# Conditioning by halves of the features, and plain float32 products for the small heads of the second block

## The chip, the cores and the metric

The kernel runs on one core of one Trainium2 chip. The metric is the device time of one execution in microseconds (us), as the median of the runs taken. Engines are named as the profile names them: PE is TensorE's matrix products and PEld its loads of the stationary operand, DVE is VectorE, ACT is ScalarE, POOL is GpSimd, SP is SyncE, which issues most transfers. In the profile "L262" is line 262 of the kernel before.

## The reference, cut

Two blocks follow each other on 256 tokens of 1024 features, all in float32, one sequence.

The first block has two hybrid layers. Each takes a conditioning vector (for the tokens and for 256 context tokens) through a 1024 x 3072 product, and gets from it a shift, a scale and a gate for every feature:

```python
shift, scale, gate = jnp.split((sc @ w_ada + b_ada)[:, None, :], 3, axis=-1)
h = rmsnorm(x, norm_w) * (1.0 + scale) + shift
```

`h` then goes through one wide projection into three branches (a gated linear recurrence in four heads, a differential attention in eight heads, a Fourier mixing), which are gated, merged, projected and added to `x` with the gate.

The second block has two layers of mixer, cross attention to 256 memory tokens with four heads of 128, and a gated feed-forward of 2816 features. The mixers differ:

- `mixer_ab` (first layer): two attentions with 8 query heads of 64 on 2 key heads each. The first normalises and rotates its queries and keys; the second only rotates them, has a window of 128 tokens and a sink term in its softmax.
- `mixer_cd` (second layer): an attention of 8 heads of 64 + 32 features whose queries, keys and values come out of low-rank factors, and a neighbourhood attention of 8 heads of 64 with a bias for each relative position.

## The kernel before

**Numbers.** A projection product is made of three products of "reduced" operands (type `F32R`): each operand is split into a high part, its value as that type holds it, and a low part, what is left; `mm3` (lines 259 to 264) multiplies high with high, high with low, low with high, and adds them in PSUM. A weight piece of 128 x 1024 values is read by SP into a ring of three raw buffers (`raw_weights`), its high part is made on ACT (L256) and its low part on DVE or on POOL (L257). The table `POOL` says for each part of the program how many such splits go to POOL: an entry `(n, s)` sends every n-th one there, and n = 0 sends none. `split` (L266 to L274) does the same with activations, always on ACT and DVE. For score products of heads with 64 features, `stack_q` and `stack_k` (L276 to L287) lay the high and the low part of 64 rows over each other in 128 rows, so that two products (`mm_stacked`, L303 and L304) do for three; the low keys stand in tiles whose other half is zero (`make_zeroed`). In the attention of 64 + 32 features and in all value products `mm3` is used.

**Order.** The first block stands in a `tc.block` whose instructions a scheduler orders by a simulated timeline; the second block is issued in the order of the code. Each engine runs its own queue in order. The transfers of weights are all issued by SP in the order of the stream, each as soon as its raw buffer is free.

**Start** (`start`, from L442). SP loads the features of tokens and context (`xT`, 2.1 MB) and 16 pieces of the conditioning weight, 0.5 MB each, in the order of the rows of that weight: two pieces make one row block of 128 input features with all 2048 columns that shift and scale need. They go through four slots in two `big` tiles. For each row block four products of 512 columns (L474), in four column groups of the array, add into one PSUM bank (`pv`), over all eight row blocks. Then the bank is copied, transposed, and the bias is added; then `hybrid_norm` normalises all eight feature blocks, one after the other, splits them, and the first projection can start.

**Conditioning inside the layers.** The gate third of the first layer and all three thirds of the second are made later, in eight places: `ada_product` (from L502) takes a group of 512 columns, reads its four pieces (two row blocks each) through the three raw buffers of the projections, runs two products of 512 columns for each piece (L510), copies the bank to SBUF on ACT, and turns and sums the four column groups by four small products with `sum4`. It is called after heads 1 and 3 of the recurrence branch and after each pair of heads of the attention branch in `hybrid`.

**`mixer_ab`** (from L1366). Token-wise projections give keys and values; keys are normalised (`head_norm`, with the inverse root L335 to L338), rotated (`rope_tok`) and transposed; values are scaled and split into high and low tiles, each head twice side by side. The queries follow, for both attentions. Then, for each of four pairs of heads and both attentions, it computes scores for two blocks of 128 queries, then the softmax and the transposition of the probabilities (`softmax_t`, L1274 to L1307; L1299 scales 256 columns, L1301 transposes), and `pair_values` (from L1312) multiplies by the values and splits the result into the `y` tiles. Between these come the projections of the memory's keys and values (`memory_now`); the output projection ends the mixer.

**`mixer_cd`** (from L1473) makes the low-rank factors first, then, for each of four pairs of heads, both attentions in turn; `near_project` makes the queries and keys of the neighbourhood attention for the next pair.

PSUM has 8 banks of 512 float32 columns for each partition; their names (`mm`, `sc`, `tp`, `pv`) stand as tile names in the profile. Buffer counts of the second block are in `SECOND`.

## Time and profile before

| | |
|---|---|
| median of 3 runs | 2439.83 us (2437.66 to 2440.39) |
| the profiled execution | 2442.6 us, of which its span is 2440.8 |
| PE busy | 2296.8 us, 94% of the span |
| PEld busy | 2066.6 us, 85% |
| DVE busy | 1617.7 us, 66% |
| ACT busy | 1163.4 us, 48% |
| POOL busy | 472.2 us, 19% |
| mean granted clock of PE | 0.977 of full speed |
| DMA | 330.87 MB, 136 GB/s in the mean |

Busy times are sums over the span, so the stages have to be told apart by time. In the trace the start is at 0 to 42 us, the first hybrid layer ends at about 1020, the second at 1661; `mixer_ab` is at 1661 to 1831, its cross attention to 1880, its feed-forward to 2062; `mixer_cd` at 2062 to 2204, its cross attention to 2255, its feed-forward to the end. The granted clock is the share of TensorE's full speed that the throttle allowed; the two levels are 1.2 and 2.4 GHz, so a mean of 0.81 over a stretch says that part of it ran at the lower one. A row of the order in time gives a start, a duration, an engine and a line; "xN" is a burst of N like instructions in one row. In a group by line, what stands behind "|" is the idle time of the engine just ahead of these instructions and what ended most of it.

### The profile page before, as it was taken

How to read it: one execution, taken by the hardware profiler on the slowest of the kernel's cores; microseconds unless marked ns; L12 is line 12 of the kernel's file. 1: busy time of each engine (PE TensorE's matmuls, PEld its weight loads, DVE VectorE, ACT ScalarE, POOL GpSimd, SP SyncE). 2: the span in 40 equal slices, each digit the busy share in tenths (PEclk: the TensorE clock that was granted, in tenths of full speed). 3: DMA queues.
4: the chain of work that ended last, by engine and by line, in shares of the span. 5: the costliest groups of instructions: out<-in, count | busy, mean ns of one | idle time of the engine just before them, and what ended most of it. 6: DMA issues, size and time to landing. Idle time of an engine off the chain costs nothing.

```text
span 2440.8 us, 40377 instructions
## 1 busy us (share of the span) xinstructions
PE 2296.8 (94%) x15566; PEld 2066.6 (85%) x15566; DVE 1617.7 (66%) x3372; ACT 1163.4 (48%) x2172; POOL 472.2 (19%) x354
## 2 busy tenths in 40 slices
PE   6999999999999999989999999898698999888998
PEld 3787878798797887779889999896588999788998
DVE  5745566466575555586557778666987766887765
ACT  3344443444554233335445666444465444665543
POOL 2422220111121102002110000123352211222221
PEclk8999999999999999999999999998899999999999
DMA  6223234323323434443445434554233555433554
GB/s 254 78 92 114 95 109 155 125 88 101 116 93 131 151 103 154 142 130 117 134 147 186 131 113 141 180 166 147 86 102 123 183 183 180 132 109 121 189 183 139
DMA packets 111072, 330.87 MB, mean 136 GB/s; under 512 B 12320, under 2 KB 24352, under 8 KB 110880
## 3 DMA queue, kind: packets, MB, share of 16 engines
q1 hardware_dynamic: 90432, 299.87, 37.5%
q10 hardware_dynamic: 20448, 28.42, 3.4%
q8 instruction: 123, 2.02, 0.4%
...
## 4 chain that ended last, share of the span: by engine, by line
PE 80%; DVE 12%; ACT 3%; DMA 3%; issue 2%; POOL 0%; ACTq 0%; SPq 0%; DVEq 0%; POOLq 0%
PE mm L262 22%; PE mm L263 22%; PE mm L264 22%; PE pv L262 2%; PE pv L263 2%; PE pv L264 2%; DVE w_low L257 1%; DVE h L274 1%; ACT w_high L256 1%; DVE e L1299 1%; DMA w_raw<-wstream 1%; PE mm L510 1%; PE sc L303 1%; DVE mx L1279 1%; PE sc L304 1%
## 5 line engine op out<-in xcount | busy, mean ns | idle before, releaser
L256 ACT CAST w_high<-w_raw 128x1024 fp32r<-128x1024 f32 (+1 forms) x490 | 508.0, 1038 | 583.1 <-PE mm L263 351.8
L257 DVE TENSOR_TENSOR w_low<-w_raw,w_high 128x1024 fp32r<-128x1024 f32 (+1 forms) x395 | 497.3, 1260 | 189.3 <-ACT w_high L256 184.8
L262 PE MATMUL mm<-big,w_high 128*128 128x512 f32 (+1 forms) x1664 | 573.3, 346 | 12.4 <-DVE g L942 5.7
L263 PE MATMUL mm<-big,w_high 128*128 128x512 f32 (+1 forms) x1664 | 571.3, 344 | 0.0
L264 PE MATMUL mm<-big,w_low 128*128 128x512 f32 (+1 forms) x1664 | 570.0, 343 | 0.0
L257 POOL TENSOR_TENSOR w_low<-w_raw,w_high 128x1024 fp32r<-128x1024 f32 x95 | 230.4, 2428 | 739.6 <-ACT w_high L256 600.3
L262 PEld LDWEIGHTS mm<-big,w_high 128*128 128x128 f32 x1664 | 316.1, 190 | 56.6 <-DVE g L942 6.1
L264 PEld LDWEIGHTS mm<-big,w_low 128*128 128x128 f32 x1664 | 316.4, 190 | 37.5 <-DVE w_low L257 0.4
L263 PEld LDWEIGHTS mm<-big,w_high 128*128 128x128 f32 x1664 | 316.6, 190 | 36.5 <-DVE big L271 0.2
L263 PE MATMUL mm<-w_low,big 128*128 128x256 f32 x960 | 269.9, 282 | 4.2 <-POOL w_low L257 2.8
L262 PE MATMUL mm<-w_high,big 128*128 128x256 f32 x960 | 268.0, 282 | 1.6 <-ACT w_high L256 1.6
L264 PE MATMUL mm<-w_high,big 128*128 128x256 f32 x960 | 268.3, 281 | 0.0
L263 PE MATMUL mm<-h,w_high 128*128 128x256 f32 x896 | 255.5, 285 | 4.8 <-DVE h L274 4.1
L262 PE MATMUL mm<-h,w_high 128*128 128x256 f32 x896 | 253.4, 284 | 2.7 <-ACT h L273 1.7
L264 PE MATMUL mm<-h,w_low 128*128 128x256 f32 x896 | 253.6, 283 | 0.0
L263 PEld LDWEIGHTS mm<-w_low,big 128*128 128x128 f32 x960 | 181.1, 189 | 6.2 <-POOL w_low L257 3.7
L262 PEld LDWEIGHTS mm<-w_high,big 128*128 128x128 f32 x960 | 180.6, 189 | 3.5 <-ACT w_high L256 2.8
L264 PEld LDWEIGHTS mm<-w_high,big 128*128 128x128 f32 x960 | 181.0, 189 | 0.4
L263 PEld LDWEIGHTS mm<-h,w_high 128*128 128x128 f32 x896 | 169.7, 189 | 7.6 <-DVE h L274 7.5
L262 PEld LDWEIGHTS mm<-h,w_high 128*128 128x128 f32 x896 | 169.5, 190 | 4.4 <-ACT h L273 2.8
L264 PEld LDWEIGHTS mm<-h,w_low 128*128 128x128 f32 x896 | 169.7, 190 | 0.1
L1649 POOL TENSOR_TENSOR x<-x,r 128x256 f32<-128x256 f32 x44 | 60.2, 1368 | 190.7 <-ACT t L1648 190.7
(475 smaller groups left out, 4388.8 us busy)
## 6 DMA issues: line engine op xcount, KB each, us to landing
...
```

The lines of the kernel that those rows point to most:

```text
L256: nc.scalar.copy(h, raw)
L257: eng.tensor_tensor(lo, raw, h.bitcast(F32), op=ALU.subtract)
L262: nc.tensor.matmul(out, a[0], b[0], start=start, stop=False)
L263: nc.tensor.matmul(out, a[0], b[1], start=False, stop=False)
L264: nc.tensor.matmul(out, a[1], b[0], start=False, stop=stop)
L274: nc.vector.scalar_tensor_tensor(lo, src, scale, h.bitcast(F32), op0=ALU.mult, op1=ALU.subtract)
L303: nc.tensor.matmul(out, q, k[0], start=start, stop=False)
L304: nc.tensor.matmul(out, q, k[1], start=False, stop=stop)
L510: nc.tensor.matmul(ps[j:j + 32], self.sc32[:, 2 * q + k], raw[:, k], start=(q < 2), stop=(q >= 2))
L1279: nc.vector.reduce_max(mx, ps2, axis=AX.X, negate=True)
L1299: nc.vector.tensor_scalar(p[:, u], p[:, u], sm[:, u:u + 1], None, op0=ALU.mult)
L1649: nc.gpsimd.tensor_tensor(g, g, rb, op=ALU.mult)
```

## The change

It has three parts.

1. **Start.** The 16 pieces of the first layer's conditioning come by column groups of 512 instead of by row blocks. A piece now holds two row blocks of one group. The order is shift of the first 512 features, scale of the first 512, shift of the last 512, scale of the last 512, and after each pair `hybrid_norm` is advanced by four feature blocks. Of each seven pieces in turn, four go through slots in one `big` tile, and three through the ring of raw buffers of the projections. The sum over the column groups is made with `sum4`, as in the layers. `hybrid_stats` and the multiplication of the features with their inverse root come after the first group's products.
2. **Conditioning in halves.** `ada_half` takes half of the row blocks of a group: two pieces, four products, each in a column group of its own, put forward by high priority with the other three tied behind the first. The first half's bank is copied to `acc`, and the second half adds it on DVE. There are 16 calls, one after each head, in place of eight.
3. **Second block.** The attentions of both mixers use plain float32 operands instead of split ones: one product for two or three. Queries, keys and values are written by ACT (or by DVE with their scale) without a low part; keys stand in pairs of half-zero tiles, one for each head of a pair; values stand in tiles with columns of zeros between the heads (`between_zeros`), so that both heads of a pair add into the same 256 columns of a bank, and `y` is split once over 128 rows. The projections stay as they are. In both mixers no split of weights goes to POOL any more, and the buffer counts in `SECOND` change.

```diff
-SECOND = dict(load=2, act=16, q=8, p=4, x=4, e=3, s=2, t=3, r=2)
+SECOND = dict(load=2, act=8, vz=4, q=8, p=3, x=4, e=3, s=2, t=3, r=2)
...
 POOL = dict(start=(2, 0), g0=(1, 0), g1=(0, 0), a0=(4, 1), a1=(0, 0), b0=(2, 1), b1=(0, 0), c0=(3, 0), c1=(3, 0),
-            merge0=(0, 0), merge1=(0, 0), t=(4, 2), e=(0, 0), ab=(1, 0), x=(3, 2), cd=(3, 1), f=(0, 0))
+            merge0=(0, 0), merge1=(0, 0), t=(4, 2), e=(0, 0), ab=(0, 0), x=(3, 2), cd=(0, 0), f=(0, 0))
...
+    def make_zeroed_halves(self, n):
+
+        self.zero_tiles, self.n_zero = [], 0
+        for i in range(n):
+            t = [self.pool.tile([P, S], F32, tag=f"kz{i}{u}", name=self.name("kz"), bufs=1) for u in range(2)]
+            for u in range(2):
+                self.nc.gpsimd.memset(t[u][64 * (1 - u):64 * (2 - u)], 0.0)
             self.zero_tiles.append(t)
...
         xc = self.xc = self.big()
-        slots = []
...
+        t = self.big().rearrange("p k c -> p (k c)").rearrange("p (n c) -> p n c", n=4)
+        slots = [t[:, q] for q in range(4)]
...
-        for k in range(KT):
-            nc.vector.tensor_tensor(xc[:, k], xc[:, k], rb, op=ALU.mult)
...
+        norm, n_piece = None, 0
+
+        def piece(g, q):
+            nonlocal n_piece
+            n_piece += 1
+            if n_piece % 7 in (0, 5, 6):
+                return self.raw_weights("w_ada", 0, 2 * q, 2, _cols(512 * g, 512))
+            n = self.stream.add("w_ada", 0, 2 * q, 2, _cols(512 * g, 512))
+            raw = slots[n_piece % 7 - 1]
+            nc.sync.dma_start(raw, self.io["wstream"][n])
+            return raw
+
+        for i in range(2):
+            for g in (i, 2 + i):
+                ps = self.bank("sc")
+                for half in range(2):
+                    raws = [piece(g, 2 * half + q).rearrange("p (k c) -> p k c", k=2) for q in range(2)]
+                    for j in range(4):
+                        nc.tensor.matmul(ps[32 * j:32 * j + 32], self.sc32[:, 4 * half + j], raws[j // 2][:, j % 2], start=(half == 0), stop=(half == 1))
+                if norm is None:
+                    rb = self.hybrid_stats()
+                    for k in range(KT):
+                        nc.vector.tensor_tensor(xc[:, k], xc[:, k], rb, op=ALU.mult)
+                    norm = self.hybrid_norm(0)
+                row = self.u("e")
+                nc.scalar.copy(row, ps)
+                pt = self.bank("tp")[:, :8]
+                for c in range(4):
+                    nc.tensor.matmul(pt[:, 2 * c:2 * c + 2], row[:, c * P:(c + 1) * P], self.sum4, start=True, stop=True)
+                for s in range(2):
+                    o = a[:, 4 * g:4 * g + 4, s]
+                    nc.vector.tensor_tensor(o, pt[:, s:8:2], self.vecs[:, b0 + 4 * g:b0 + 4 * g + 4], op=ALU.add)
+                    if g >= 2:
+                        nc.vector.scalar_tensor_tensor(o, o, 1.0, self.vec("norm_w0")[:, 4 * i:4 * i + 4], op0=ALU.add, op1=ALU.mult)
+            for _ in range(4):
+                next(norm)
+        next(norm, None)
         self.load_consts(CUT_1, self.base, "xres")
...
-    def ada_group(self, l, groups):
-        for g in groups:
-            self.ada_product(l, g)
-
-    def ada_product(self, l, g):
+    def ada_half(self, l, g, half):
 
         nc = self.nc
         ps = self.mm()
-        for q in range(4):
-            raw = self.raw_weights("w_ada", l, 2 * q, 2, _cols(512 * g, 512)).rearrange("p (k c) -> p k c", k=2)
-            for k in range(2):
-                j = 32 * (2 * (q % 2) + k)
-                nc.tensor.matmul(ps[j:j + 32], self.sc32[:, 2 * q + k], raw[:, k], start=(q < 2), stop=(q >= 2))
+        raw = [self.raw_weights("w_ada", l, 4 * half + 2 * q, 2, _cols(512 * g, 512)).rearrange("p (k c) -> p k c", k=2) for q in range(2)]
+
+        def product(j):
+            return nc.tensor.matmul(ps[32 * j:32 * j + 32], self.sc32[:, 4 * half + j], raw[j // 2][:, j % 2], start=True, stop=True)
+
+
+        with self.tc.high_priority():
+            first = product(3)
+            with self.tc.issue_after(first.ins if hasattr(first, "ins") else first):
+                for j in range(3):
+                    product(j)
+        if half == 0:
+            nc.scalar.copy(self.acc, ps)
+            return
         row = self.u("y")
-        nc.scalar.copy(row, ps)
+        nc.vector.tensor_tensor(row, ps, self.acc, op=ALU.add)
...
-            if hd in (1, 3):
-                self.ada_group(l, range(4 + hd // 2, 5 + hd // 2))
+            self.ada_half(l, 4 + hd // 2, hd % 2)
...
                 if last_end:
                     last_end()
+                if l == 0:
+                    self.ada_half(1, pair, u)
                 self.merge_gates(GATES_B)
-            if l == 0:
-                self.ada_group(1, range(pair, pair + 1))
...
-        if whole:
+        if not isinstance(pts, tuple):
+            nc.scalar.copy(pts[:, :, :, sl], pt)
+        elif whole:
             self.split(pts[0][:, :, :, sl], pts[1][:, :, :, sl], pt)
...
-    def pair_values(self, y, k, pts, vs):
-
-        po = self.bank("pv").rearrange("p (u c) -> p u c", u=2)
+    def between_zeros(self, n):
+
+        v = self.u("vz", [P, 64 * (2 * n + 1)])
+        self.nc.gpsimd.memset(v[:, :P * n].rearrange("p (g c) -> p g c", c=P)[:, :, :64], 0.0)
+        self.nc.gpsimd.memset(v[:, P * n:], 0.0)
+        return v, v[:, 64:].rearrange("p (g c) -> p g c", c=P)[:, :, :64]
+
+    def pair_values(self, y, k, pts, v, heads):
+
+        po = self.bank("pv")[:, :S]
         for u in range(2):
-            m = 64 * (u + 1)
+            lo = P * heads[u] + 64 * (1 - u)
             for s in range(2):
-                vh, vl = vs(u, s)
-                self.mm3(po[:m, u], (vh, vl), (pts[0][:, u, s], pts[1][:, u, s]), s == 0, s == 1)
-            rows = slice(64 * u, 64 * u + 64)
-            self.split(y[0][rows, k, :S], y[1][rows, k, :S], po[rows, u])
+                self.nc.tensor.matmul(po, v[s][:, lo:lo + P], pts[:, u, s], start=u == 0 and s == 0, stop=u == 1 and s == 1)
+        self.split(y[0][:, k, :S], y[1][:, k, :S], po)
...
+    def key_tile(self, src):
+
+        k = self.zeroed()
+        for u in range(2):
+            self.nc.scalar.copy(k[u][64 * u:64 * u + 64], src[64 * u:64 * u + 64])
+        return k
...
             nc.scalar.activation(kx, pss[t][:, :256], AF.Copy, scale=r[:, t:t + 1])
-            v = tuple(self.u("act", dt=F32R) for _ in range(2))
...
+            v, at = self.between_zeros(4)
+            nc.scalar.activation(at, pss[t][:, 256:].rearrange("p (g c) -> p g c", c=64), AF.Copy, scale=r[:, t:t + 1])
             vv.append(v)
...
+            kv = kr.rearrange("p (g u c) -> p g u c", u=2, c=64)
+            for i, (kx_, rn) in enumerate(((ka, "r2"), (kb, "r1"))):
+                self.rope_tok([kv[:, 2 * i + g, 0].unsqueeze(1) for g in range(2)], kx_, tab[rn + "_c"][:, t], tab[rn + "_s"][:, t], 2, 32)
+                nc.scalar.copy(kv[:, 2 * i:2 * i + 2, 1], kv[:, 2 * i:2 * i + 2, 0])
...
-        for src in (kt_ps, kt_ps2):
...
+                nc.tensor.transpose((kt_ps, kt_ps2)[g // 2][:, (g % 2) * S + t * P:(g % 2) * S + (t + 1) * P], kr[:, P * g:P * g + P], self.ident)
+
+        kT = [[self.key_tile(src[:, g * S:(g + 1) * S]) for g in range(2)] for src in (kt_ps, kt_ps2)]
...
-                qT[kind].append([self.u("q", dt=F32R) for _ in range(2)])
-                for u in range(2):
-                    self.stack_q(qT[kind][i][u], ptq[i][64 * u:64 * u + 64])
+                qT[kind].append(self.u("q"))
+                nc.scalar.copy(qT[kind][i], ptq[i])
...
-                pts = self.new_pts()
+                pts = self.u("p", [P, 2, 2, S])
...
-                        self.mm_stacked(ps[:, u], qT[kind][pr // 2][u][:, qsl], tuple(x[:, ksl] for x in kT[kind]), kind == 0, kind == 0 or u == 1)
+                        nc.tensor.matmul(ps[:, u], qT[kind][pr // 2][:, qsl], kT[kind][g][u], start=kind == 0, stop=kind == 0 or u == 1)
...
-                self.pair_values(y, 4 * kind + pr, pts, vs)
+                self.pair_values(y, 4 * kind + pr, pts, vv, (2 * kind + g,) * 2)
...
-            t = self.u("x")[:, :S]
-            self.nc.vector.tensor_tensor(t, ps, rb, op=ALU.mult)
...
+            if j == 0:
+                q = self.u("q")[:, :S]
+                self.nc.vector.tensor_tensor(q, ps, rb, op=ALU.mult)
+            else:
+                k = self.zeroed()
+                for u in range(2):
+                    sl = slice(64 * u, 64 * u + 64)
+                    self.nc.vector.tensor_tensor(k[u][sl], ps[sl], rb[sl], op=ALU.mult)
+        return q, k
...
-                v = tuple(self.u("act", dt=F32R) for _ in range(2))
-                self.split(v[0], v[1], pss[t], scale=r[:, t:t + 1])
+                v, at = self.between_zeros(8)
+                nc.scalar.activation(at, pss[t].rearrange("p (g c) -> p g c", c=64), AF.Copy, scale=r[:, t:t + 1])
...
-            c = tuple(self.u("p", [P, 2, S], F32R) for _ in range(2))
+            c = tuple(self.u("q", [P, 2, S], F32R) for _ in range(2))
...
+            v, at = self.between_zeros(8)
+            nc.scalar.copy(at, ps.rearrange("p (g c) -> p g c", c=64))
...
-                a, b = (self.u("q", [P, 2, S], F32R)[:96] for _ in range(2))
-                self.split(a, b, pt)
-                pair.append((a, b))
-            pts = self.new_pts()
+                a = self.u("q", [P, 2, S])[:96]
+                nc.scalar.copy(a, pt)
+                pair.append(a)
...
+            pts = self.u("p", [P, 2, 2, S])
             for qi in range(2):
                 ps = self.bank("sc").rearrange("p (u c) -> p u c", u=2)
                 for u in range(2):
-                    a, b = pair[u]
-                    qsl = slice(qi * P, (qi + 1) * P)
-                    self.mm3(ps[:, u], (a[:, 0, qsl], b[:, 0, qsl]), (a[:, 1], b[:, 1]), True, True)
+                    nc.tensor.matmul(ps[:, u], pair[u][:, 0, qi * P:(qi + 1) * P], pair[u][:, 1], start=True, stop=True)
                 self.softmax_t(ps, pts, qi)
-            self.pair_values(y, pr, pts, lambda u, s, pr=pr: tuple(x[:, P * pr:P * pr + 64 * (u + 1)] for x in vc[s]))
-
-            pts = self.new_pts()
+            self.pair_values(y, pr, pts, vc, (2 * pr, 2 * pr + 1))
...
+            pts = self.u("p", [P, 2, 2, S])
...
-                    self.mm_stacked(ps[:, u * S:(u + 1) * S], qk[u][:, qi * P:(qi + 1) * P], qk[2 + u])
+                    nc.tensor.matmul(ps[:, u * S:(u + 1) * S], qk[0][:, qi * P:(qi + 1) * P], qk[1][u], start=True, stop=True)
...
+            self.pair_values(y, 4 + pr, pts, vd, (2 * pr, 2 * pr + 1))
...
-            a = self.u("act" if f < 16 else "q", [P, 2, S], F32R)
+            if f % 2 == 0 and f < 8:
+                two = self.u("vz", [P, 2, 2, S], F32R)
+            a = two[:, f % 2] if f < 8 else self.u("act" if f < 16 else "q", [P, 2, S], F32R)
```

## Rows read from the trace of the kernel before

**Rows 1.** Page, part 1: busy us (share of the span) xinstructions.

```profile
PE 2296.8 (94%) x15566; PEld 2066.6 (85%) x15566; DVE 1617.7 (66%) x3372; ACT 1163.4 (48%) x2172; POOL 472.2 (19%) x354
```

**Rows 2.** Stretches: busy us by engine, clock, DMA; sums of eight and 26.

```profile
1178.00:1195.00 17.00, 15.44 (x86) 11.60 (x85) 10.55 (x25) 8.68 (x20) 3.49 (x4) 0.81 0.61 202
sum 115.00, PE 96.02 PEld 66.14 DVE 57.68 ACT 61.01 POOL 22.34; mean PE 12.00 PEld 8.27 DVE 7.21 ACT 7.63 POOL 2.79
...
sum 833.00, PE 825.14 PEld 711.88 DVE 490.39 ACT 346.62 POOL 147.29; mean PE 31.74 PEld 27.38 DVE 18.86 ACT 13.33 POOL 5.66
```

**Rows 3.** Stretches of the two mixers, columns as before.

```profile
1679.00:1738.00 59.00, 40.45 (x169) 31.82 (x167) 49.15 (x101) 23.39 (x40) 24.19 (x10) 0.83 0.33 107
1738.00:1797.00 59.00, 46.18 (x297) 39.86 (x297) 55.11 (x131) 38.75 (x116) 16.75 (x8) 0.94 0.17 54
...
2100.00:2180.00 80.00, 67.63 (x476) 60.33 (x475) 65.66 (x127) 59.70 (x156) 18.04 (x14) 0.94 0.35 113
```

**Rows 4.** Groups by line, 1660 to 1830 us: busy us, mean ns | idle before.

```profile
L1299 DVE TENSOR_SCALAR e<-e,sm 128x256 f32<-128x256 f32 x32 | 20.1, 663 | 0.2
L274 DVE SCALAR_TENSOR_TENSOR h<-xres,vecs,h 128x256 fp32r<-128x256 f32 x15 | 17.9, 1225 | 3.9 <-ACT h L273 3.9
L271 DVE TENSOR_TENSOR p<-tp,p 128x512 fp32r<-128x512 f32 x16 | 10.7, 682 | 1.4 <-ACT p L270 1.3
L338 DVE TENSOR_TENSOR hn_r_t<-hn_r_t,hn_r_v 128x2 f32<-128x2 f32 x6 | 7.4, 1236 | 0.2
...
L257 POOL TENSOR_TENSOR w_low<-w_raw,w_high 128x1024 fp32r<-128x1024 f32 x26 | 62.4, 2403 | 98.6 <-ACT w_high L256 89.3 <-DMA load<-rpb 5.6 <-PE pv L264 3.8
```

**Rows 5.** Chain of waits, 1738 to 1840 us: start us, us, what.

```profile
1774.82 0.22 PE tp L1301 x2
1784.54 0.52 DVE e L1299 x2
```

**Rows 6.** Order in time, 1680 to 1700 us: start us, us, engine, line.

```profile
1681.95 2.37 POOL L257 TENSOR_TENSOR w_low<-w_raw,w_high 128x1024 fp32r<-128x1024 f32 x1 [0.43 <-ACT w_high L256]
1681.97 2.36 DVE L338 TENSOR_TENSOR hn_r_t<-hn_r_t,hn_r_v 128x2 f32<-128x2 f32 x1
1684.76 0.16 DVE L338 TENSOR_TENSOR hn_r_t<-hn_r_t,hn_r_v 128x2 f32<-128x2 f32 x1
1685.03 0.48 DVE L274 SCALAR_TENSOR_TENSOR act<-mm,rstd,act 128x256 fp32r<-128x256 f32 x1
```

**Rows 7.** Stretch from 4 to 40 us, columns as in rows 2.

```profile
4.00:40.00 36.00, 21.09 (x84) 6.65 (x84) 21.45 (x56) 9.65 (x15) 7.86 (x3) 0.91 1.03 400
```

**Rows 8.** Order in time, 37 to 43 us.

```profile
37.81 1.05 PE L474 MATMUL pv<-big,sc 128*32 128x512 f32 x4 [0.23 <-DMA big<-wstream]
42.15 0.79 PE L262 MATMUL pv<-big,w_high 128*128 128x512 f32 x1 [1.89 <-ACT big L270]
```

**Rows 9.** Order in time, TensorE, 216 to 226 us.

```profile
216.49 1.91 PE L510 MATMUL mm<-w_raw,sc 128*32 128x512 f32 x12
221.72 1.05 PE L510 MATMUL mm<-w_raw,sc 128*32 128x512 f32 x4 [1.02 <-DMA w_raw<-wstream]
```

**Rows 10.** Chain of waits, 216 to 226 us.

```profile
216.56 1.02 PE mm L510 x8
217.59 4.09 DMA w_raw<-wstream
```

**Rows 11.** Order in time, TensorE, 2300 to 2303 us.

```profile
2300.40 0.28 PE L262 MATMUL mm<-h,w_high 128*128 128x256 f32 x1
2300.51 0.28 PE L263 MATMUL mm<-h,w_high 128*128 128x256 f32 x1
```

**Rows 12.** Order in time, TensorE, 803 to 806 us.

```profile
803.31 1.05 PE L357 MATMUL tp<-ident,b_rs 128*128 128x128 f32 x8
804.12 0.48 PE L264 MATMUL mm<-big,w_low 128*128 128x512 f32 x1
```

**Rows 13.** Order in time, TensorE, 1140 to 1180 us.

```profile
1144.74 0.69 PE L872 MATMUL sc<-negm,ident 4*128 4x256 f32 x2
```

58 lines of the change are left out of this document (3 added, 55 removed).

## The prediction

> **What bounds the kernel now.** I read the engine totals and slices first: TensorE is busy 94% of the span, so only a stretch in which it stands still or runs slowly can give time back [rows 1]. The table by stretch says where these are. Most of the first block is not among them: in 26 stretches of it, 833 us, TensorE is busy for 825 [rows 2]. What is left is the start (no projection product until 42 us), the eight places where a conditioning product of 512 columns runs (TensorE busy 96.0 us of 115) [rows 2], and the mixers of the second block: `mixer_ab` from 1679 us on, where VectorE is busy 49 of 59 us and then 55 of 59, and the attention part of `mixer_cd`, where it is busy 66 of 80 [rows 3]. Then I grouped what VectorE does there. Its scaling of 256 columns (L1299) takes 663 ns in the mean, the 2-column step L338 of the inverse root 1236 ns (a second row, of 8 columns, has six more of 1252) [rows 4], while undisturbed ones take 0.26 us (two in 0.52 in the chain [rows 5]) and 0.16. The order in time shows why: GpSimd starts a split of 2.37 us at 1681.95, VectorE starts a 2-column step at 1681.97, and both end together; the next step of that form takes 0.16 us [rows 6]. So a GpSimd split holds a VectorE step that comes behind it for the split's whole length. The profiled run took 2442.6 us (span 2440.8); the median of the runs is 2439.8, 2.8 less. The sum is made against 2442.6.
>
> **Start.** The transfers run at 400 GB/s from 4 to 40 us without a gap [rows 7], so bytes set this part. The last of 16 conditioning pieces is used at 37.81, and the first product with a projection weight starts at 42.15 [rows 8]. Now every piece has to be there before the first feature is normalised. After: features (2.1 MB), vectors (0.35) and 16 pieces (8.4) are 10.9 MB; with 0.5 MB moved by 4 us they are there at 4 + 10.4/0.40 = 30 us. The first half is there at 4 + 6.1/0.40 = 19 us, and its four features are multiplied and split (about 1.5 us each on VectorE) while the second half arrives. The first weight follows at 31, its cast takes 1 us, so products start at about 33, with 4 features times 3 products in up to 4 banks to do (48 products, 11 us) while the other features come, at 33 to 38. That is 9 us earlier. Bounds: 3 us if the constants, memory and three weights stand in front as they do now (then only the normalisation is hidden), 14 if weights come between the halves. The 64 records of this conditioning on TensorE stay and lie under the transfers.
>
> **Conditioning in halves.** A product now takes a burst of 12 records (1.91 us) and a burst of 4 (1.05) for the fourth piece, which needs the buffer of the first [rows 9]: the chain shows 4.09 us for that transfer at 217.59 [rows 10]. Afterwards a half has two pieces for which three buffers are there, and its four products, in four column groups, make one burst of 8 records, which takes 1.02 us now [rows 10]. TensorE: from 8 x 2.96 = 23.7 to 16 x 1.05 = 16.8 us, 6.9 less. Idle: 19.0 us now [rows 2]. But the half's first product, put forward by high priority, stands at the head of TensorE's queue, and all projection products behind it, and the casts and evictions that wait for them, are late if the second piece is. The waits of that kind seen are 0 to 1.65 us; I take 0.8 for each of 16, 13 us, so 6 less. A granted clock below 1 at three of the eight, as at 1178 (0.81) [rows 2], gives about 1 more. Sum 14 less; bounds 24 less (idle 4, clock full) and 4 more (16 waits of 1.8 and no clock regained). The eight additions of 512 columns that VectorE gets for ACT copies (6 us) have cover in the first block, where it is busy some 60%; without cover they cost 6.
>
> **The plain float32 products.** Today three (or two, stacked) reduced products of 256 columns start every 0.117 us [rows 11]; 512 columns take twice that. A plain product shows as two records: eight records of 128 columns (four products) take 1.05 us, and the next product starts 0.81 us after the first of them [rows 12]; doubled to 256 columns that is 0.41 to 0.52 us each, while the two records L872 of 256 columns and 4 rows take 0.69 [rows 13]. I take 0.44, near the first since its operands are of full height, and keep 0.41 and 0.69. Counts are from the loops. `mixer_ab`: 64 score products become 32 (7.5 to 14.1 us), 96 value products become 32 (11.2 to 14.1): 9.5 more. `mixer_cd`: 48 become 16, 32 become 16, 96 become 32: 20.6 to 28.2, 7.6 more. TensorE pays 17 us; at 0.69 it is 49.
>
> **What `mixer_ab` gets for it.** VectorE loses 16 subtractions L271 of 512 columns (10.7 us [rows 4]), and by the durations of such sizes 12 us more on `y`, `q`, `kz` and the values: 23. GpSimd's 26 splits of 2.40 us move to it at about 1.27, 33 us. The stalls go: L1299 20.1 against 32 x 0.26, L274 on `xres` 17.9 against 15 x 0.48 [rows 6], both rows of L338 14.9 against 12 x 0.17, about 35 us, and 42 with smaller ones [rows 4]. So VectorE is relieved by 23 + 42 - 33 = 32 us, but TensorE then sets the stage. From 1679 to 1738 VectorE's chain rules: 49.2 less 18.6 of those stalls, less 6.1 removed, plus 10 splits (12.3) is 37, with 8 of gaps 45: 14 less than 59. From then TensorE has scores 14.1, masks 1.8, transposes 7 (two in 0.22 [rows 5]), values 14.1, memory products 22.5 and the output projection 22.5: 82 us, and 6 for the first and last links make 88, against 93 now. Together 20 less (bounds 8, with the chain giving 8 and the dearest product eating the rest, and 30). New ACT copies (keys in halves, doubled `kr`) equal those removed. The memsets of value tiles have no row; they are few, on a GpSimd that is freed of 62 us: nothing, and at most 2 us per mixer if each stalls VectorE once as long as its own split would.
>
> **`mixer_cd`.** In its attention stretch VectorE drops 20 us of subtractions of the same forms, some 4 in the near projections and 5.6 of stalls, and takes about 4 splits (5): 66 to some 41. TensorE has about 61 us of work there by the same rates; with gaps the stretch takes 68 instead of 80. A microsecond more comes from splits in the first part that stall small steps. 13 less, bounds 4 (product at 0.69) and 20.
>
> **Sum.** 9 + 14 + 20 + 13 = 56: 2442.6 - 56 = 2387 against the profiled run, 2384 against the median. `act` with 8 tiles and `vz` with 4 hold the arrays that 16 held. One `p` tile fewer touches `cross` alone, where a late low part would wait for one value product, under 1 us. I count both at nothing.
>
> **A rule against it.** The page Perfetto Trace Analysis of the Trainium skill (Optimizing Scalar/DVE Operations) says that a saturated DVE may gain by offloading work to GpSimd, though it warns of a port that both share. By its first half, taking 36 splits back onto a VectorE that is 93% busy loses time; the trace so far bears out the warning, with 42 us of stalls [rows 4, 6], and cannot show the other side.
>
> **Rivals.** (1) VectorE becomes the bound: 36 splits at 1.27 us, 45 us, land in front of the chains' small steps, and both mixers stay as long as now. Then 23 us are gained: 2417. For it: 55 of 59 us [rows 3]. Against it: the pair at 1681.95 [rows 6]. (2) The start and the halves do nothing, since as many bytes stand in front of the last feature and each half waits for its piece: 33 us gained, 2407. For it: the full transfers [rows 7]. (3) Slower: the half's first product, at the head of TensorE's queue, waits for a whole transfer. At the 4.09 us of 217.59, 16 halves lose 66 us, and a clock that drops after each, at 1.5 us, 24 more; less the 26 of today's conditioning and 42 from elsewhere that is 2462. It decides from 2.8 us per half with that clock, 4.3 without. Against it: three raw buffers for two pieces. (4) The plain products cost 0.69 each: 32 us more, 2416.
>
> **How the numbers follow.** Forecast 2384, chance 0.66 (2360 to 2402); the second rival 0.14; the first and fourth together 0.14; slower 0.04; no change 0.02. The range leaves out slower and no change and thin tails on both sides: 2356 to 2419. Faster by over 0.2% (5 us, about what a measurement of this kernel can tell) 0.94, within 0.02, slower 0.04.
>
> **What would show it.** First projection product near 33 us; L510's successor in 16 bursts of about 1.05 us, with under 1 us of idle in front; L338 and L1299 in `mixer_ab` at 0.17 and 0.26 us; no GpSimd splits there; score products of about 0.44 us; TensorE above 95% from the first scores to the end of the output projection. Wrong would be: VectorE over 90% busy in `mixer_ab`, conditioning products waiting 2 us or more for a transfer, plain products above 0.6 us.

## The result and the profile after

The changed kernel takes 2377.26 us in the median of 4 runs (2375.91 to 2379.83); the kernel before took 2439.7 beside it. The ratio is 0.9747, with a 95% interval of 0.973 to 0.9764. The forecast was 2384, with 2356 to 2419 as its range. The profiled execution took 2378.5 us (span 2376.7), 64.1 less than the one of before, for a sum of 56.

The totals of the page of the changed kernel answer to [rows 1]: TensorE is busy for 9 us less in a span 64 us shorter, GpSimd for 71 us less.

```profile
PE 2287.5 (96%) x15514; PEld 2064.3 (87%) x15514; DVE 1562.9 (66%) x3340; ACT 1146.0 (48%) x2137; POOL 401.4 (17%) x336
```

To see where 64 us went I cut both traces at the end of the last residual addition of each stage on VectorE (L1262 before, L1288 after; for the first block the last L1006 or its successor). In the trace of the changed kernel the last addition of the first mixer is this one; it ends at 1780.0.

```profile
1779.58 0.42 DVE L1288 TENSOR_TENSOR xres<-mm,xres 128x256 f32<-128x256 f32 x1
```

Lengths of the stages in us, worked out in this way for every profiled execution that the text needs (names of the experiments as below):

| kernel | first block | `mixer_ab` | cross | feed-forward | `mixer_cd` | cross | feed-forward |
|---|---|---|---|---|---|---|---|
| before | 1661.2 | 167.9 | 43.4 | 188.0 | 138.2 | 44.2 | 188.1 |
| after | 1633.5 | 146.5 | 43.8 | 187.6 | 123.6 | 43.8 | 187.6 |
| halves_only | 1631.8 | 164.6 | 43.4 | 189.2 | 137.7 | 44.3 | 188.0 |
| second_only | 1660.3 | 147.0 | 43.4 | 187.7 | 123.9 | 43.5 | 187.6 |
| pool_only | 1657.2 | 144.0 | 42.3 | 188.0 | 132.8 | 43.5 | 188.0 |
| plain_pool_back | 1630.6 | 166.0 | 43.5 | 187.7 | 127.1 | 43.6 | 187.7 |
| ab_split | 1631.0 | 144.2 | 42.5 | 187.6 | 123.5 | 43.7 | 187.7 |
| pool_none | 1627.0 | 147.1 | 40.8 | 187.7 | 123.4 | 40.8 | 187.7 |
| both | 1627.2 | 144.1 | 40.8 | 187.7 | 123.5 | 40.8 | 187.7 |

So 27.7 us came in the first block (start and halves), 21.4 in `mixer_ab`, 14.6 in `mixer_cd`. One pair of traces leaves some 3 us open in `mixer_ab`: with the second block of before it took 167.9 us in the trace of before, but 164.6 in that of halves_only and 164.3 in that of start_only. Against these two the gain in `mixer_ab` is 18 us. The row of halves_only for this stage (from, to, us, then busy us of PE, PEld, DVE, ACT, POOL, clock, DMA):

```profile
1631.80:1796.40 164.60, 131.09 (x765) 112.39 (x765) 132.67 (x280) 89.33 (x199) 70.32 (x34) 0.91 0.32 108
```

**The start.** Order in time, changed kernel; it answers to [rows 8]:

```profile
27.09 0.33 SPq L563 DMA_DIRECT2D load<-memT  x1
34.65 1.82 PE L493 MATMUL sc<-big,sc 128*32 128x512 f32 x4 [0.67 <-DMA big<-wstream]
38.23 4.70 POOL L257 TENSOR_TENSOR w_low<-w_raw,w_high 128x1024 fp32r<-128x1024 f32 x2 [35.59 <-ACT w_high L256]
38.92 0.77 PE L262 MATMUL pv<-big,w_high 128*128 128x512 f32 x1
40.65 3.72 DVE L674 TENSOR_SCALAR s<-big,ada 128x256 f32<-128x256 f32 x5
```

The first projection product (L262) comes at 38.92 for 42.15. The last conditioning piece is used at 34.65, not at 30: SP put the constants (at 10.15) and memory transfers (the second at 27.09) between the pieces. Two GpSimd splits then run for 4.70 us from 38.23, and VectorE's normalisation of the second half of the features (L674) stretches beside them.

**The halves and the plain products.** Order in time of the changed kernel: a burst of a conditioning half, which answers to [rows 9], and a burst of eight records (four value products) in plain float32. The row after it is from the chain of waits, which follows the same burst without the pipeline's overlap at its end.

```profile
212.19 1.06 PE L527 MATMUL mm<-w_raw,sc 128*32 128x512 f32 x8
1704.49 1.89 PE L1353 MATMUL pv<-p,vz 128*128 128x256 f32 x8
```

```profile
1704.65 1.73 PE pv L1353 x8
```

All 16 halves are bursts of 1.06 to 1.07 us, and no conditioning product waits for a transfer: the view of line 527 has 3.9 us of idle time in front of them in all, 3.3 of it without a releaser. A plain product of 256 columns takes 1.73 / 4 = 0.43 us.

**VectorE in `mixer_ab`.** Groups by line, 1633 to 1783 us (busy us, mean ns), which answer to [rows 4]:

```profile
L274 DVE SCALAR_TENSOR_TENSOR h<-xres,vecs,h 128x256 fp32r<-128x256 f32 x16 | 11.4, 745 | 0.8 <-ACT h L273 0.8
L1325 DVE TENSOR_SCALAR e<-e,sm 128x256 f32<-128x256 f32 x32 | 10.0, 349 | 0.4
L347 DVE TENSOR_TENSOR hn_r_t<-hn_r_t,hn_r_v 128x2 f32<-128x2 f32 x6 | 1.0, 159 | 0.2
```

The 2-column step fell from 1236 to 159 ns, the scaling of 256 columns from 663 to 349, the undisturbed step in this count; the 0.26 us of [rows 5] leave out the part in which two in a row overlap. Most of the stalls are gone, as forecast. The scaling of the residual fell from 1225 only to 745, where 0.48 us was forecast. The order in time shows it stretched beside another GpSimd instruction that stayed, the addition of 256 columns L388:

```profile
1761.27 0.48 DVE L274 SCALAR_TENSOR_TENSOR h<-xres,vecs,h 128x256 fp32r<-128x256 f32 x1
1763.77 1.07 POOL L388 TENSOR_TENSOR acc<-acc,t 128x256 f32<-128x256 f32 x1 [71.79 <-ACT t L387]
1764.16 0.96 DVE L274 SCALAR_TENSOR_TENSOR h<-xres,vecs,h 128x256 fp32r<-128x256 f32 x1
```

Whether the plain products had a part in the gain, this trace can't say, since both edits came together.

### The profile page after: what moved, and what is told of

It reads as the page before. It is cut to its first block, busy times and chain, and to the rows that moved or that the text cites. A ratio compares the mean times of both kernels' runs of the same rounds, so it can differ in the third digit from the quotient of the medians.

```text
span 2376.7 us, 40209 instructions
## 1 busy us (share of the span) xinstructions
PE 2287.5 (96%) x15514; PEld 2064.3 (87%) x15514; DVE 1562.9 (66%) x3340; ACT 1146.0 (48%) x2137; POOL 401.4 (17%) x336
## 4 chain that ended last, share of the span: by engine, by line
PE 85%; DVE 6%; ACT 3%; DMA 3%; issue 1%; POOL 0%; ACTq 0%; SPq 0%; DVEq 0%; POOLq 0%
PE mm L262 24%; PE mm L263 24%; PE mm L264 24%; PE pv L263 1%; PE pv L262 1%; PE pv L264 1%; DVE w_low L257 1%; ACT w_high L256 1%; PE pv L1353 1%; PE sc L312 1%; PE tp L366 1%; PE sc L313 1%; PE tp L1182 1%; PE tp L1327 1%; PE mm L527 1%
## 5 line engine op out<-in xcount | busy, mean ns | idle before, releaser
L257 DVE TENSOR_TENSOR w_low<-w_raw,w_high 128x1024 fp32r<-128x1024 f32 (+1 forms) x429 | 533.7, 1245 | 221.6 <-ACT w_high L256 218.0
L262 PE MATMUL mm<-big,w_high 128*128 128x512 f32 (+1 forms) x1664 | 573.8, 346 | 14.9 <-ACT y L978 4.7
L262 PEld LDWEIGHTS mm<-big,w_high 128*128 128x128 f32 x1664 | 315.9, 190 | 60.4 <-ACT s L1212 5.6
L262 PE MATMUL mm<-w_high,big 128*128 128x256 f32 x960 | 267.9, 281 | 0.0
L262 PE MATMUL mm<-h,w_high 128*128 128x256 f32 x896 | 253.5, 284 | 4.6 <-ACT h L273 2.0
L257 POOL TENSOR_TENSOR w_low<-w_raw,w_high 128x1024 fp32r<-128x1024 f32 x61 | 148.4, 2434 | 542.5 <-ACT w_high L256 466.7
L262 PEld LDWEIGHTS mm<-w_high,big 128*128 128x128 f32 x960 | 179.7, 188 | 1.2
L262 PEld LDWEIGHTS mm<-h,w_high 128*128 128x128 f32 x896 | 168.4, 188 | 6.2 <-ACT h L273 2.9
L918 POOL TENSOR_TENSOR e<-e,s 128x256 f32<-128x256 f32 (+3 forms) x68 | 65.1, 969 | 178.8 <-ACT e L917 178.7
```

The lines of the kernel that those rows point to most:

```text
L257: eng.tensor_tensor(lo, raw, h.bitcast(F32), op=ALU.subtract)
L262: nc.tensor.matmul(out, a[0], b[0], start=start, stop=False)
L918: nc.gpsimd.tensor_tensor(e, e, place(sc, s, lo, hi), op=ALU.mult)
```

## The experiments

Each kernel was timed in five rounds beside the kernel before on the same chip; ratios are to that kernel, with a 95% interval. A difference of two runs is made from their ratios, times 2439 us.

### The parts alone

**start_only** is the kernel before with `start` of the changed one.

```diff
-                n = self.stream.add("w_ada", 0, k, 1, _cols(CW * i, CW))
...
-        for _ in self.hybrid_norm(0):
-            pass
...
+            n = self.stream.add("w_ada", 0, 2 * q, 2, _cols(512 * g, 512))
...
+        for i in range(2):
+            for g in (i, 2 + i):
...
+            for _ in range(4):
+                next(norm)
```

> The kernel before with the new start alone (pieces by columns, first half of the features first). Theory A, from aligning the two traces by the number of projection products done: the first product starts 3.2 us earlier, but by 140 us both traces have done the same work within 1 us, because TensorE then waits for the gate chain of the first recurrence and runs at the lower clock behind it. It gives 0 to 3 us: 2437 to 2440. Theory B: the start moves all later transfers forward, so part of the gain seen at the conditioning products comes from here: 8 us or more, 2431 or less.

Measured: 2443.3 us, ratio 1.002 (1.0007 to 1.0034). It is not faster; if anything 2 to 8 us slower, which neither theory had. Counting the projection products done by a given time, its trace is between 2 and 3 us ahead at 60 us, about 1 at 120, level with the one of before at 1520, and 2.4 behind at the end of the first block (1663.6 for 1661.2). The loss comes between 1526 and 1590 us, far from the start; what makes it is open.

**halves_only** is the kernel before with the 16 calls.

```diff
-            if hd in (1, 3):
-                self.ada_group(l, range(4 + hd // 2, 5 + hd // 2))
+            self.ada_half(l, 4 + hd // 2, hd % 2)
...
+                if l == 0:
+                    self.ada_half(1, pair, u)
                 self.merge_gates(GATES_B)
-            if l == 0:
-                self.ada_group(1, range(pair, pair + 1))
```

> The kernel before with the conditioning in halves alone (16 calls of two pieces in place of 8 of four). Theory A: the wait for the fourth piece goes with the burst of 12 records and the second of 4, TensorE loses 6.9 us of records and 15 us or more of idle time, and the clock that fell behind these waits stays up: 24 to 29 us, 2411 to 2416. Theory B: the new start had moved the transfers forward, and the halves alone wait as I forecast, 0.8 us each: 14 us, 2426.

Measured: 2409.62 us, ratio 0.9885 (0.9868 to 0.9903), 28 us. Theory A: the halves alone give all that the first block gained. What TensorE did from 130 us to the end of the first block stands in the sums of the stretches (length, then busy us by engine), of the kernel before:

```profile
sum 1531.00, PE 1484.05 PEld 1321.86 DVE 972.36 ACT 712.49 POOL 226.76; mean PE 371.01 PEld 330.46 DVE 243.09 ACT 178.12 POOL 56.69
```

and of halves_only:

```profile
sum 1502.00, PE 1471.48 PEld 1317.77 DVE 969.12 ACT 712.01 POOL 232.20; mean PE 367.87 PEld 329.44 DVE 242.28 ACT 178.00 POOL 58.05
```

29 us shorter: TensorE is busy for 12.6 us less and idle for 16.4 less (47.0 to 30.5).

**second_only** has the second block of the changed kernel behind the first block of before.

```diff
-SECOND = dict(load=2, act=16, q=8, p=4, x=4, e=3, s=2, t=3, r=2)
+SECOND = dict(load=2, act=8, vz=4, q=8, p=3, x=4, e=3, s=2, t=3, r=2)
...
-            merge0=(0, 0), merge1=(0, 0), t=(4, 2), e=(0, 0), ab=(1, 0), x=(3, 2), cd=(3, 1), f=(0, 0))
+            merge0=(0, 0), merge1=(0, 0), t=(4, 2), e=(0, 0), ab=(0, 0), x=(3, 2), cd=(0, 0), f=(0, 0))
...
-                self.make_zeroed(4)
+                self.make_zeroed_halves(4)
...
-    def pair_values(self, y, k, pts, vs):
+    def pair_values(self, y, k, pts, v, heads):
```

> The kernel before with the changes of the second block alone (plain float32 products, no weight splits on GpSimd in the two mixers). Theory A: the second block stands alone behind the first, so its gain is the 21 us of the first mixer and the 15 us of the second that the traces show: 36 us, 2404. Theory B: a part of it depends on what is loaded ahead at the end of the first block, and alone it gives under 30 us, 2410 or more.

Measured: 2404.99 us, ratio 0.9867 (0.9849 to 0.9884), 32 us; by stages 20.9 and 14.3 against the trace of before. That lies between the theories: the interval, 28 to 37 us, holds A's 36 and the upper end of B. With start_only and halves_only the three parts alone make 5 - 28 - 32 = -55 of the -62 measured together; the rest lies inside the intervals.

### What a conditioning piece holds up

**halves_together** calls both halves of a group one behind the other at the eight old places.

```diff
-            self.ada_half(l, 4 + hd // 2, hd % 2)
+            if hd in (1, 3):
+                for u in range(2):
+                    self.ada_half(l, 4 + hd // 2, u)
...
-                if l == 0:
-                    self.ada_half(1, pair, u)
                 self.merge_gates(GATES_B)
+            if l == 0:
+                for u in range(2):
+                    self.ada_half(1, pair, u)
```

> The changed kernel with both halves of a group called one behind the other at the eight old places. Four pieces are wanted within one call again, with three buffers. Theory A: the wait for a transfer in front of the second half comes back at most of the eight places, 1 to 2.5 us each with the lower clock behind it: 8 to 20 us slower than the changed kernel, 2385 to 2397. Theory B: the bursts of 8 records and the priority did it, and the distance between halves is nothing: 2375 to 2380.

**no_priority** leaves the order of a half's four products to the scheduler.

```diff
-        with self.tc.high_priority():
-            first = product(3)
-            with self.tc.issue_after(first.ins if hasattr(first, "ins") else first):
-                for j in range(3):
-                    product(j)
+        for j in range(4):
+            product(j)
```

> The changed kernel, the four products of a conditioning half issued in their plain order, without the high priority and without being tied behind the last of them. Theory A: what counts is that a half needs two pieces while three buffers are there; the scheduler finds a place of the products in any case, but bursts may break in two: 0 to 6 us slower, 2377 to 2383. Theory B: the priority is what keeps TensorE from waiting, and without it half of the gain of the halves goes: 12 us or more, 2389 or more.

Measured: halves_together 2393.16 us, ratio 0.9815 (0.9795 to 0.9836), 17 us slower than the changed kernel: the size of theory A. But not in its place: the conditioning products of that trace wait for a transfer for 0.5 us in all. no_priority 2382.62 us, ratio 0.9778 (0.9754 to 0.9801), 8 us slower, between the theories, with an interval that just overlaps that of the changed kernel. In its profiled execution only 2.3 us of this show in the first block (1635.8 us for 1633.5).

A likely place is SP's queue. These rows are from the waits of the queue of weight transfers (L242) from 130 to 1300 us, for raw buffers that conditioning products still hold: us in total, times, longest. The kernel before, halves_together, no_priority, the changed kernel, and halves_only:

```profile
SPq L242 <- PE mm L510: 139.1, 22, 19.6
```

```profile
SPq L242 <- PE mm L527: 130.5, 15, 17.7
```

```profile
SPq L242 <- PE mm L527: 53.6, 19, 7.0
```

```profile
SPq L242 <- PE mm L527: 27.5, 11, 4.7
```

```profile
SPq L242 <- PE mm L505: 27.0, 10, 5.0
```

A piece of conditioning lies in one of the three raw buffers until its products have had their turn on TensorE. When that buffer's turn comes, SP, which issues in order, can't send for the next weights, up to 19.6 us at a stretch before. The two kernels with the short first block have 27 us of this wait, the two with the long one over 130, no_priority lies between. But the sum is not the time lost: SP waits for raw buffers most of the time in every one of these kernels, and all its L242 rows together make 1027 us (before), 1021, 1026, 1009 and 1010 of the 1170 us. What sets the slow two apart is who holds the buffer and how long at a stretch: 19.6 and 17.7 us, where no single wait of the other three is over 14.2. So this queue as the cause fits the runs and is not shown; a kernel with a fourth raw buffer, which would test it, was not run. What TensorE then waits for is named otherwise at each place: a cast of a late weight, a softmax that had no projection to hide it. In the sum of the stretches halves_together (130 us to the end of the first block) is idle for 39.8 us of 1517, 9 more than halves_only, and busy for 6 more.

```profile
sum 1517.00, PE 1477.19 PEld 1322.85 DVE 979.81 ACT 713.57 POOL 223.97; mean PE 369.30 PEld 330.71 DVE 244.95 ACT 178.39 POOL 55.99
```

So it is the distance between two halves that counts: without it 17 of the 28 us are lost. For the priority the two intervals leave anything from about nothing to some 15 us.

### The mixers: who made the gain

**pool_only** changes two entries of the table and nothing else.

```diff
-            merge0=(0, 0), merge1=(0, 0), t=(4, 2), e=(0, 0), ab=(1, 0), x=(3, 2), cd=(3, 1), f=(0, 0))
+            merge0=(0, 0), merge1=(0, 0), t=(4, 2), e=(0, 0), ab=(0, 0), x=(3, 2), cd=(0, 0), f=(0, 0))
```

> The kernel before with one table entry changed in each mixer of the second block: no split of weights on GpSimd there, all on VectorE; products and values as before. Theory A: the stalls behind GpSimd's splits (some 42 us of VectorE in the first mixer and 19 in the second) cost more than the 33 and 12 us of splits that VectorE takes over, and VectorE's chain sets both stages: 6 to 16 us faster, 2424 to 2434. Theory B: the splits on VectorE land in front of the small steps of the chain and eat it all, or more: no change or slower, 2438 to 2455; then the plain products are what made room.

**plain_pool_back** is the changed kernel with these entries as before.

```diff
-            merge0=(0, 0), merge1=(0, 0), t=(4, 2), e=(0, 0), ab=(0, 0), x=(3, 2), cd=(0, 0), f=(0, 0))
+            merge0=(0, 0), merge1=(0, 0), t=(4, 2), e=(0, 0), ab=(1, 0), x=(3, 2), cd=(3, 1), f=(0, 0))
```

> The changed kernel with weight splits of both mixers of the second block back on GpSimd as before (all of the first mixer's, every third of the second's). Theory A: the stalls of VectorE's small steps come back, but VectorE has fewer subtractions to do and TensorE more products, so it costs less than the stalls' sum: 5 to 20 us slower than the changed kernel, 2382 to 2397. Theory B: the plain products made the room and the place of the splits no longer matters: 2375 to 2380.

**ab_split** is the changed kernel with the split operands of before in `mixer_ab`, four `p` tiles, and the splits on VectorE.

```diff
-SECOND = dict(load=2, act=8, vz=4, q=8, p=3, x=4, e=3, s=2, t=3, r=2)
+SECOND = dict(load=2, act=8, vz=4, q=8, p=4, x=4, e=3, s=2, t=3, r=2)
...
+            vt = self.u("vz", [P, 2, 512], F32R)
+            v = vt[:, 0], vt[:, 1]
...
+        kh, kl = (self.u("vz", [P, 2, 512], F32R) for _ in range(2))
...
-                        nc.tensor.matmul(ps[:, u], qT[kind][pr // 2][:, qsl], kT[kind][g][u], start=kind == 0, stop=kind == 0 or u == 1)
+                        self.mm_stacked(ps[:, u], qT[kind][pr // 2][u][:, qsl], kT[kind][g], kind == 0, kind == 0 or u == 1)
...
-                self.pair_values(y, 4 * kind + pr, pts, vv, (2 * kind + g,) * 2)
+                self.pair_values_split(y, 4 * kind + pr, pts, vs)
```

> The changed kernel with the split (three and two product) operands of the kernel before in the first mixer of the second block; weight splits on VectorE there, the second mixer plain as changed. Theory A, from the stage lengths of the runs so far (144.0 us with the table entry alone, 146.5 with the plain products too): once the splits are off GpSimd, TensorE sets this mixer, and the plain products cost it 9.5 us of which 2 to 8 show: 2369 to 2375. Theory B: VectorE sets it still, and the 23 us of subtractions that come back make it 5 us slower or more: 2382 to 2395.

Measured: pool_only 2410.53 us, ratio 0.9894 (0.9877 to 0.9912), 26 us faster than before and more than theory A had. plain_pool_back 2399.06 us, ratio 0.9839 (0.9819 to 0.986), 22 us slower than the changed kernel, just past theory A's end. ab_split 2373.4 us, ratio 0.9742 (0.9728 to 0.9755): 1 us faster than the changed kernel by the ratios, which is no difference by itself, but `mixer_ab` in its trace is 2.3 us shorter, the same 144 us as in pool_only.

The whole of `mixer_ab`, as one stretch (us, then busy us of PE, PEld, DVE, ACT, POOL, clock, DMA). The kernel before:

```profile
1661.00:1829.00 168.00, 133.28 (x764) 113.93 (x765) 134.31 (x279) 89.27 (x199) 70.12 (x34) 0.89 0.32 105
```

pool_only, the table alone:

```profile
1657.00:1801.00 144.00, 125.94 (x754) 107.97 (x755) 124.83 (x304) 88.51 (x199) 11.05 (x9) 0.91 0.37 122
```

plain_pool_back, the plain products without the table:

```profile
1630.60:1796.60 166.00, 140.68 (x733) 117.18 (x733) 113.01 (x246) 84.48 (x193) 71.33 (x37) 0.90 0.32 106
```

the changed kernel, with both:

```profile
1633.50:1780.00 146.50, 131.03 (x722) 110.81 (x723) 108.30 (x269) 84.32 (x193) 12.54 (x11) 0.93 0.37 120
```

Here is the case in four lines. From the first to the second VectorE takes over 25 splits (it makes 27 now, 33.6 us by its group below, where it made two in 2.7 us), and is busy for 9.5 us less; 24 us are gained, or 20 against the two other traces with the second block of before. From the first to the third VectorE is relieved of 21 us by the plain products, and the stage is 2 us shorter, or 1 to 2 longer than in those two: nothing that can be told from none. From the second to the fourth it is relieved of 16.5 us again, TensorE has 5.1 more, and the stage is 2.5 us longer. That is little, but it repeats: of the traces without GpSimd splits in this stage, the three with split operands (pool_only, ab_split, both) take 144.0 to 144.3 us in it, the seven with plain ones 146.5 to 148.8.

A split on GpSimd takes twice as long as on VectorE, so the gain could also come from low parts that TensorE gets sooner. The chain of waits speaks against it. In the kernel before it has no GpSimd split in this stage, and no wait of TensorE there was ended by one; VectorE has 102 of its 167 us, the stalled steps in front. In pool_only VectorE has 32 of 144. The beginnings of its sums by line, the kernel before and then pool_only:

```profile
by line: DVE e L1299 9.8%; DVE h L274 9.6%; DVE hn_r_t L338 8.6%; PE mm L264 7.6%; PE mm L262 7.2%; PE mm L263 6.8%; DVE mx L1279 4.9%; issue 4.4%; DVE p L271 3.0%; DVE q L280 2.5%; DVE t L1330 2.4%; ACT h L273 2.3%; DVE x L1337 1.9%; DVE t
```

```profile
by line: PE mm L263 12.1%; PE mm L262 11.9%; PE mm L264 11.7%; DVE w_low L257 6.5%; ACT w_high L256 5.5%; issue 5.3%; ACT e L1286 3.8%; PE tp L1301 3.8%; DMA w_raw<-wstream 3.7%; DMA load<-memT 3.2%; DVE h L274 2.9%; PE sc L303 2.1%; PE pv 
```

Once the stalls are gone, VectorE's own work hardly sets this stage any more, and taking it away buys nothing here.

The groups of pool_only, 1657 to 1801 us, show the same step lengths as the changed kernel, without a plain product:

```profile
L257 DVE TENSOR_TENSOR w_low<-w_raw,w_high 128x1024 fp32r<-128x1024 f32 x27 | 33.6, 1244 | 9.0 <-ACT w_high L256 8.8
L271 DVE TENSOR_TENSOR p<-tp,p 128x512 fp32r<-128x512 f32 x16 | 10.8, 687 | 0.7 <-ACT p L270 0.2
L1299 DVE TENSOR_SCALAR e<-e,sm 128x256 f32<-128x256 f32 x32 | 10.0, 347 | 0.1
L338 DVE TENSOR_TENSOR hn_r_t<-hn_r_t,hn_r_v 128x2 f32<-128x2 f32 x6 | 0.9, 158 | 0.1
```

In `mixer_cd` it is otherwise: by the table of stages the entry alone gives 5.4 us, the plain products alone 10.6 (halves_only to plain_pool_back), both 14.6. That fits a stage in which VectorE's own subtractions, and not stalls, were the larger part of its chain, since only every third split was on GpSimd; this I read from the counts and did not test further.

### The start, and the splits elsewhere

**no_start** is the changed kernel with the start of before.

```diff
-            n = self.stream.add("w_ada", 0, 2 * q, 2, _cols(512 * g, 512))
...
-            for _ in range(4):
-                next(norm)
...
+                n = self.stream.add("w_ada", 0, k, 1, _cols(CW * i, CW))
...
+        for _ in self.hybrid_norm(0):
+            pass
```

> The changed kernel with the start of the kernel before (pieces by rows, all features normalised at its end); the rest as changed. Theory A, from the run with the new start alone (no faster than before): the earlier first product is lost again by 140 us, so the start is worth nothing: 2373 to 2379. Theory B: beside the halves the new start is worth its 3 us, and the kernel is 2 to 5 us slower: 2379 to 2382.

Measured: 2374.75 us, ratio 0.9753 (0.9736 to 0.9771), against 0.9747: no difference. The first block ends at 1633.0 us, against 1633.5. The new start is worth nothing that shows here.

**late_consts** makes SP issue the constants and two memory transfers behind the last piece that goes through a slot.

```diff
+            self.last_piece = d.ins if hasattr(d, "ins") else d
...
-        self.load_consts(CUT_1, self.base, "xres")
+        with self.tc.issue_after(self.last_piece):
+            self.load_consts(CUT_1, self.base, "xres")
...
+                with self.tc.issue_after(self.last_piece):
                     self.b_setup()
...
+                with self.tc.issue_after(self.last_piece):
                     self.memory_stats()
```

> The changed kernel, SP issuing the constants, the lambda vectors and the first memory transfers (1.28 MB until 28 us) behind the last of the conditioning pieces that go through the slots. Theory A: bytes set the start, at 0.40 MB per us, so the last piece lands 3 us earlier (31.5 us for 34.6) and the first projection product starts at some 36 us; at the end of the kernel 0 to 3 us are left of it: 2374 to 2378. Theory B: constants that come late hold up the gate chain of the first recurrence, and the kernel is 1 to 6 us slower: 2378 to 2383.

Measured: 2377.78 us, ratio 0.9753 (0.9732 to 0.9773): no difference. The order in time has the last conditioning products in a burst that ends at 32.86, 3.6 us before that of the changed kernel (34.65 + 1.82):

```profile
30.27 2.59 PE L494 MATMUL sc<-big,sc 128*32 128x512 f32 x8
```

so bytes do set the arrival. But the chain of waits goes elsewhere:

```profile
23.63 10.10 DMA consts<-consts
33.76 0.23 DVE rope_c L1074
```

VectorE's queue is in order, and the products for the rotation tables (L1074) stand in front of the second half of the features: they wait for the constants until 33.73. The first projection product starts at 37.04, for 38.92: about half of what the pieces gained, the constants take.

**pool_none** takes the last 62 splits off GpSimd.

```diff
-POOL = dict(start=(2, 0), g0=(1, 0), g1=(0, 0), a0=(4, 1), a1=(0, 0), b0=(2, 1), b1=(0, 0), c0=(3, 0), c1=(3, 0),
+POOL = dict(start=(0, 0), g0=(0, 0), g1=(0, 0), a0=(0, 0), a1=(0, 0), b0=(0, 0), b1=(0, 0), c0=(0, 0), c1=(0, 0),
...
-            merge0=(0, 0), merge1=(0, 0), t=(4, 2), e=(0, 0), ab=(0, 0), x=(3, 2), cd=(0, 0), f=(0, 0))
+            merge0=(0, 0), merge1=(0, 0), t=(0, 0), e=(0, 0), ab=(0, 0), x=(0, 0), cd=(0, 0), f=(0, 0))
```

> The changed kernel with no split of weights on GpSimd anywhere: the 55 of the first block and the seven of the cross attentions and others go to VectorE too. Theory A, that a GpSimd split holds VectorE's small steps wherever they meet: but TensorE is busy 1585 of the 1633 us before the first mixer, so only part of the 48 us of idle time and of the clock behind it can come back: 2 to 12 us faster, 2365 to 2375. Theory B: VectorE has cover in the first block, and 55 splits of 1.25 us on it come in front of the low parts that TensorE waits for: 0 to 15 us slower, 2377 to 2392.

Measured: 2368.61 us, ratio 0.9722 (0.9708 to 0.9735), 6 us faster than the changed kernel, with intervals that just touch. Theory A. By the stages 3 us come in each cross attention (43.8 to 40.8; 42.3 is the shortest in the traces with the splits there), which had two splits each, and 6.5 in the first block; the two profiled executions differ by more than the medians. In the start, order in time:

```profile
37.49 0.50 PE L262 MATMUL pv<-big,w_high 128*128 128x512 f32 x1
40.10 2.03 DVE L674 TENSOR_SCALAR s<-big,ada 128x256 f32<-128x256 f32 x6
```

Six steps L674 take 2.03 us, where five took 3.72 beside the two splits. TensorE's granted clock was at its full level from 38 to 48 us in this execution (1.00) and not in that of the changed kernel (0.65), so not all of the 7 us of work by which this trace is ahead of that of before at 120 us (the changed kernel: 0.8) belong to the splits.

**both** joins pool_none and ab_split.

```diff
-SECOND = dict(load=2, act=8, vz=4, q=8, p=3, x=4, e=3, s=2, t=3, r=2)
+SECOND = dict(load=2, act=8, vz=4, q=8, p=4, x=4, e=3, s=2, t=3, r=2)
...
-            merge0=(0, 0), merge1=(0, 0), t=(4, 2), e=(0, 0), ab=(0, 0), x=(3, 2), cd=(0, 0), f=(0, 0))
+            merge0=(0, 0), merge1=(0, 0), t=(0, 0), e=(0, 0), ab=(0, 0), x=(0, 0), cd=(0, 0), f=(0, 0))
```

> The two edits that were each faster than the changed kernel put together: no split of weights on GpSimd anywhere, and the split operands of the kernel before in the first mixer. Theory A: they act in different stages (the start, the cross attentions and the layers; the first mixer), so their gains add: ratio to the kernel before 0.971 or a little less, 2363 to 2368. Theory B: with the splits of the start and of the layers on VectorE the first mixer has none of its gain left: 2368 to 2372.

Measured: 2365.57 us, ratio 0.9697 (0.9684 to 0.971), 12 us faster than the changed kernel and the fastest kernel of the study. Theory A: `mixer_ab` 144.1, cross attentions 40.8, first block 1627.2. At 120 us its trace is 3.6 us of work ahead of that of before, with a granted clock of 0.68 from 38 to 48 us, where the changed kernel has 0.65 and is 0.8 ahead. At like clocks, then, some 3 us are gained by 120 us without GpSimd splits. Whether those beside the start or those of the first layer behind it make the difference is not told apart, and the other traces with the start of before differ by up to 1.7 us at that point.

## Why the prediction was right, step by step

- **Stalls behind GpSimd splits: right, and more than I made of them.** I saw the pair at 1681.95 [rows 6], priced the stalls of `mixer_ab` at 42 us and the splits at 33, so 9 net. Measured by pool_only: VectorE 9.5 us less, at 1.24 us for a split where I had 1.27. But the stage gave 20 to 24 us for these 9: it is by the chain that it is set, and the stalls sat there (VectorE 102 us of the chain before, 32 after), while of the splits 9 us stand on it.
- **`mixer_ab`, -20 (its two parts, 14 and 5, make 19): measured -21.4, or -18 against the two other traces, for a reason that was only half the one given.** The step that failed is that the 23 us of subtractions belong to the gain. They do not: plain products alone give nothing that shows, beside the table they cost 2.5. My own sentence that TensorE then sets the stage was right, and should have led me to ask what the plain products are for in it.
- **Price of a plain product, 0.44 taken: 0.43 measured.** Rival 4 (0.69) falls. The page FP8 and Floating Point Precision of the Trainium skill (TensorE Precision Notes) counts true FP32 as four passes; by the 0.117 us of a reduced product [rows 11] that is an estimate of 0.47, and the trace has 0.43.
- **`mixer_cd`, -13: measured -14.6**, with the plain products as the larger part, as the sum had it.
- **Halves, -14 with -24 as the far bound: measured -28.** The failed term is "0.8 for each of 16, 13 us": no half waits for its piece. Without this term the sum would have been 27. By halves_only the idle time fell by 16.4 us where I had 6, and TensorE's busy time by 12.6 where I had 8 with the clock. Of the idle time of before [rows 2] only 3.9 us were TensorE waiting for a conditioning piece (four waits, one of them in [rows 9]). For the rest the long waits of SP's queue for buffers with conditioning pieces in them are the likely cause, not a shown one; I had read only TensorE's waits. Rival 3 (each half waits for a whole transfer) falls, and rival 2 for the halves; for the start rival 2 was right.
- **Start, -9 with -3 as the near bound: nothing.** The first product did come 3.2 us earlier, with constants and memory in front "as they do now"; I had taken that for the bound and the other for the likely case, though the change does not touch them. In the changed kernel nothing of these 3.2 us reaches the end; that GpSimd splits beside and behind the start take them is what `both` and pool_none suggest, not more.
- **Rival 1, VectorE becomes the bound:** falls; in the stretch from 1698 to 1749 us, from about the first scores to the end of the attentions, TensorE is busy 50.28 of 51 us and VectorE 34.72.

```profile
1698.00:1749.00 51.00, 50.28 (x287) 42.50 (x286) 34.72 (x108) 33.90 (x106) 0.00 (x0) 1.00 0.08 25
```

- **Rule against the change:** that a loaded VectorE gains by giving work to GpSimd does not hold here: pool_only gave the work back, in a stage with VectorE 93% busy in one stretch (55.11 of 59 us [rows 3]), and gained. What the runs bear out is what the page SBUF — State Buffer of the Trainium skill states (Who interferes with whom): of a VectorE step with two SBUF inputs, or in a two-port mode, and a GpSimd instruction that reads SBUF, the one that is issued first holds the shared port for its whole length. By that rule a 2-column step costs a whole split, and the rows agree: 2.36 us beside one [rows 6], 0.16 without. One step of before with an input in PSUM (`mm`) was not held; it took 0.48 us beside a split, as the same step does without one [rows 6]:

```profile
1679.10 2.41 POOL L257 TENSOR_TENSOR w_low<-w_raw,w_high 128x1024 fp32r<-128x1024 f32 x1 [0.35 <-ACT w_high L256]
1680.25 0.48 DVE L274 SCALAR_TENSOR_TENSOR act<-mm,rstd,act 128x256 fp32r<-128x256 f32 x1 [10.48 <-ACT act L273]
```

So the total was near in part by luck: an error of 14 us in the halves stood against one of 9 in the start, and two edits that I had priced together in `mixer_ab` came as a pair.
